# A decoder layer on one core: weight tiles of the seven-product stage that last for the stage and are loaded by halves

## The chip, the core and the metric

The kernel runs on one core of a Trainium2 chip. The metric is the device time of one execution in microseconds; the time before is the median of three runs. Times inside the execution are read from one profiled execution and counted from its start.

## What is computed

The reference is one decoder layer on 512 tokens of width 2048, all float32. Only its end matters for the change:

```python
x = layer_norm(DEEPNORM_ALPHA * x + mix, ln_mix_g[layer], ln_mix_b[layer])
f = jnp.square(jax.nn.relu(x @ w_ff1[layer])) @ w_ff2[layer]
x = layer_norm(DEEPNORM_ALPHA * x + f, ln_ff_g[layer], ln_ff_b[layer])
```

`w_ff1` is 2048 x 8192, `w_ff2` 8192 x 2048. The change touches only `x @ w_ff1`.

## The kernel before

**Precision.** Every float32 product is made of three matmuls on a faster 32-bit format: each operand is split into a high part (written by ScalarE, L87) and the rest (written by VectorE, L88), and high x high, high x low and low x high are added up in PSUM. So each weight half that TensorE uses goes through ScalarE and then VectorE first. The split parts of weights are called wh and wl; each has three buffers.

**The seven-product stage.** `x @ w_ff1` is cut into 16 groups of 512 columns. The first group is computed plainly. The other 15 are units (class `FUnit`): each takes its 2048 x 512 weights as a 2 x 2 matrix of four tiles of 1 MB, 1024 x 256 each, called "11", "12", "21" and "22", and the activations as 2 x 2 as well, and computes the product with seven block products (ORDER, M1 to M7) where eight would be plain. The price is sums of weight tiles on VectorE (`FUnit.sum`, L612), which are made in place, half a tile at a time: 11 += 12, 11 += 22, 12 += 22, 11 += 21.

**Pieces.** Each product has two pieces, one for each half of its weight tile; a unit has 14, j = 0 to 13, and a piece is 24 matmuls of 256 columns (L652). Products by piece: j 0 and 1 use "11"; 2 and 3 "11" after 11 += 12; 4 and 5 "11" after 11 += 22; 6 and 7 "22"; 8 and 9 "12" after 12 += 22; 10 and 11 "21"; 12 and 13 "11" after 11 += 21.

**The order of the work** is written out by hand. In front of the matmuls of piece j stand the split of piece j + 2 (with the sums 11 += 12 and 11 += 22 for the first four pieces) and what `beside` lists for j. That holds the sums 12 += 22 (j 4 and 6) and 11 += 21 (j 8 and 9), the evacuation of PSUM to the tile R (`block`, L661 on VectorE; L617 to L619 and L664 on ScalarE), and for the unit before: additions in R (L548) and its output to DRAM, `h_parts_out`, at j 5 and j 7. That output splits R into hpH (a high part in one buffer, ScalarE, L87) and the rest in R itself (VectorE, L88), and GpSimd's queue writes both to h_parts (L555), 896 KB each. GpSimd's queue also carries three loads of 256 KB of the other work of the stage (y_load) at j 7. Each engine and each queue runs its own instructions in the order written.

**Four tiles and their hand-over.** SBUF holds only four weight tiles at a time. When a unit has used one up, it hands its place to the next unit, whose tile is then loaded by SyncE's queue (L608, one transfer of 1 MB):

```python
        elif j == 6:
            act(u2, u.ps["M1"], AF.Copy, scale=-1.0)
            u.sum("12", "22", 1)
            u.give("22", u.order[0])
        elif j == 7:
            u.give("12", u.order[1])
```

`order` is "11", "12", "22", "21": the place of "22" takes the next "11" (at j 6), that of "12" the next "12" (j 7), that of "21" the next "22" (j 9) and that of "11" the next "21" (j 11). In the trace all these tiles are named w. The load waits until all readers of the old tile are done.

Of the kernel before, what the change touches and what calls it, by code (L numbers as in the profile page):

```python
# [9 lines left out]
F32 = mybir.dt.float32  # L10
# [6 lines left out]
P = 128  # L17
# [51 lines left out]
def decoder_layer(ctx: ExitStack, tc: tile.TileContext, x, xt, positions, w_in, w_pool, pool_scale,  # L69
                  w_branch_attn, w_branch_pool, w_out, ln_mix_g, ln_mix_b, w_ff1, w_ff2,  # L70
                  ln_ff_g, ln_ff_b, consts, vectors, out, h_parts, h_rest, y_norm, y_parts):
    nc = tc.nc
# [364 lines left out]
    L2 = {}  # L437
# [78 lines left out]
    def y_load(t, n):  # L516
        c = slice(n * 512, (n + 1) * 512)
        nc.gpsimd.dma_start(low["u"][:, 1], y_norm[t, :, c])
        nc.gpsimd.dma_start(low["g"][:, 0], bcast(ln_mix_g, c))
        nc.gpsimd.dma_start(low["g"][:, 1], bcast(ln_mix_b, c))  # L520
# [51 lines left out]
    def ff1_evac(g):  # L572

        def f(b, p):
            if not R:
# [8 lines left out]
    ORDER = ("M1", "M5", "M6", "M3", "M7", "M2", "M4")  # L584
    FACTORS = {"M1": ("11", "11"), "M5": ("P1", "11"), "M6": ("P2", "11"), "M3": ("P4", "22"), "M7": ("P3", "12"),
               "M2": ("12", "21"), "M4": ("22", "11")}
    low = {}

    def yblock(who, k):

# [7 lines left out]
    class FUnit:  # L598
# [3 lines left out]
            self.rest = None  # L602
            self.g, self.b, self.tag, self.next, self.ps, self.out = g, {}, {}, None, {}, h_out(g)

        def get(self, role):
            self.b[role] = L2["p"].tile([P, 8, 256], F32, name="w1", tag=self.tag[role])
            k, c0 = int(role[0]) - 1, self.g * 512 + (2 - int(role[1])) * 256
            nc.sync.dma_start(self.b[role], w_ff1[k * 1024:(k + 1) * 1024, c0:c0 + 256].rearrange("(a p) n -> p a n", p=P))  # L608

        def sum(self, role, other, half):  # L610
            c = slice(4 * half, 4 * half + 4)
# [6 lines left out]
                nc.scalar.activation(R[self.g][:, :, 2], self.ps["M1"].rearrange("p (n t) -> p n t", n=2), AF.Relu)  # L618
                nc.scalar.activation(R[self.g][:, :, :4], R[self.g][:, :, :4], AF.Square)  # L619

        def give(self, role, new):
            self.next.tag[new] = self.tag[role]
            self.next.get(new)

    class FPiece:
        def __init__(self, unit, j):
# [27 lines left out]
    def beside(u, j, last):  # L654

        v = {m: p.rearrange("p (n t) -> p n t", n=2) for m, p in u.ps.items()}
        m1, m5, u2 = low["m"][:, 0], low["m"][:, 1], low["u"][:, 0]
        act = nc.scalar.activation

        def block(slot, in0, in1, op):  # L660
            nc.vector.tensor_tensor(R[u.g][:, :, slot], in0.rearrange("p (n t) -> p n t", n=2), in1, op=op)  # L661

        def relu(a, b):
            act(R[u.g][:, :, a:b], R[u.g][:, :, a:b], AF.Relu)  # L664

        if j == 0:
            last.done()
        elif j == 2:
            act(m1, u.ps["M1"], AF.Copy)
        elif j == 4:  # L670
            act(m5, u.ps["M5"], AF.Copy, scale=-1.0)
            u.sum("12", "22", 0)
        elif j == 6:
            act(u2, u.ps["M1"], AF.Copy, scale=-1.0)
            u.sum("12", "22", 1)
            u.give("22", u.order[0])
        elif j == 7:
            u.give("12", u.order[1])
            if chunks:
                y_load(*chunks[0])  # L680
        elif j == 8:
            u.sum("11", "21", 0)
        elif j == 9:
            u.sum("11", "21", 1)
            u.give("21", u.order[2])
        elif j == 10:
            block(0, m5, v["M1"], OP.subtract)
        elif j == 11:
            u.give("11", u.order[3])
            if chunks:  # L690
                u.rest = y_rows(*chunks.pop(0))
        elif j == 12:
            block(1, u2, v["M5"], OP.subtract)
        elif j == 13:
            block(3, m1, v["M2"], OP.add)
            relu(0, 2)
        if j == 3 and last.rest:
            last.rest()
        if j in last.out:
            last.out[j]()  # L700
# [190 lines left out]
    units = [Unit(c, u) for c in range(7) for u in range(2)]  # L891
# [30 lines left out]
    p = PS.tile([P, 512], F32, name="mm", bufs=6)  # L922
# [170 lines left out]
```

## Time and profile before

| what | us |
|---|---|
| median of three runs | 2491.09 |
| lowest and highest of them | 2490.66, 2492.37 |
| the profiled execution | 2494.17 |
| its span in the profile | 2492.4 |
| TensorE busy in the span | 2418.1 (97%) |
| VectorE busy | 1585.7 (64%) |
| ScalarE busy | 960.9 (39%) |
| mean granted clock of TensorE | 0.985 |

The span is what lies between the first and the last instruction of the profile; 1.8 us lie around it. A busy engine is not an engine at its best: TensorE counts as busy while it runs at half its clock. So beside the busy time the granted clock and the number of matmuls in a stretch have to be read. PE is TensorE, DVE VectorE, ACT ScalarE, POOL GpSimd, SP SyncE, whose queue issues the loads of weights.

### The profile page before, as it was taken

To read this page: it belongs to the slowest core of one execution; us is meant where nothing else is said; L and a number is where in the kernel's file an instruction comes from. 1 tells how busy PE (TensorE), PEld (TensorE's weight loads), DVE (VectorE), ACT (ScalarE), POOL (GpSimd) and SP (SyncE) were. 2 spreads that over 40 slices of the span, in tenths; PEclk is the share of its full clock that TensorE was granted. 3 is DMA by queue.
4 is the path that set the end of the run, shared out by engine and by line. 5 is a ranking of instruction groups with operands and counts; after the bars stand their busy time and mean duration, and the time that the engine had idled before them with its cause. 6 is when DMAs were issued, how large, how long until landed. Compare 5 with 4: busy or idle time off the path is not lost.

```text
span 2492.4 us, 31596 instructions
## 1 busy us (share of the span) xinstructions
PE 2418.1 (97%) x13096; PEld 2101.9 (84%) x13096; DVE 1585.7 (64%) x1641; ACT 960.9 (39%) x1030; POOL 168.7 (7%) x256
## 2 busy tenths in 40 slices
PE   9999999999999999998998998999999999999998
PEld 7888888877788888888998998999988888888886
DVE  4532254555532333367877877878868889888886
ACT  4323311244422232156445545545454433333330
POOL 0000000000000000000111110111121001110000
PEclk9999999999999999999999999999999999999999
DMA  6232333322223333365676575674688566665652
GB/s 204 86 93 97 110 93 102 93 77 76 77 93 96 99 99 127 114 205 173 189 234 203 172 236 175 188 234 158 223 288 285 177 213 234 205 227 172 218 167 95
DMA packets 201919, 399.32 MB, mean 160 GB/s; under 512 B 11312, under 2 KB 73904, under 8 KB 201008
## 3 DMA queue, kind: packets, MB, share of 16 engines
q1 hardware_dynamic: 163312, 257.83, 32.2%
q0 software_dynamic: 36160, 135.28, 16.1%
q10 hardware_dynamic: 2304, 4.20, 0.5%
q8 instruction: 102, 1.67, 0.3%
q14 instruction: 41, 0.34, 0.0%
HBM read 329.11 MB, written 68.16 MB: 159 GB/s over the span
## 4 chain that ended last, share of the span: by engine, by line
PE 75%; DMA 11%; DVE 8%; issue 3%; ACT 2%; POOLq 0%; SPq 0%; DVEq 0%; ACTq 0%
PE mm L147 42%; PE pp L785 21%; DMA w<-in_w_ff 10%; PE mm L652 5%; DVE wl L88 4%; PE pp L830 3%; DVE w L612 1%; ACT wh L87 1%; DVE hpR L88 1%; DVE hpR L548 1%; PE sc L351 1%; PE tp L383 1%; DMA part<-y_parts 1%; DVE hpR L661 1%; DMA wr<-in_w_out 0%
## 5 line engine op out<-in xcount | busy, mean ns | idle before, releaser
L88 DVE TENSOR_TENSOR wl<-wr,wh 128x1024 fp32r<-128x1024 f32 (+1 forms) x228 | 277.4, 1219 | 570.6 <-ACT wh L87 569.9
L87 ACT ACTIVATE wh<-w 128x1024 fp32r<-128x1024 f32 x406 | 426.1, 1058 | 542.7 <-PE pp L785 296.3
L88 DVE TENSOR_TENSOR wl<-w,wh 128x1024 fp32r<-128x1024 f32 x406 | 494.2, 1220 | 151.7 <-ACT wh L87 149.8
L785 PE MATMUL pp<-wh,hop 128*128 128x512 f32 x1568 | 483.0, 389 | 1.2 <-ACT hpR L618 1.2
L87 ACT ACTIVATE wh<-wr 128x1024 fp32r<-128x1024 f32 (+1 forms) x228 | 240.4, 1055 | 616.1 <-PE mm L147 571.7
L147 PE MATMUL mm<-aH,wh 128*128 128x512 f32 (+1 forms) x1024 | 395.5, 386 | 1.8 <-ACT wh L87 1.8
L147 PE MATMUL mm<-aH,wl 128*128 128x512 f32 (+1 forms) x1024 | 386.8, 378 | 5.1 <-DVE wl L88 5.1
L147 PE MATMUL mm<-aL,wh 128*128 128x512 f32 (+1 forms) x1024 | 385.6, 377 | 0.0
L785 PEld LDWEIGHTS pp<-wh,hop 128*128 128x128 f32 x1568 | 294.3, 188 | 62.3 <-ACT hpR L618 1.4
L652 PE MATMUL mm<-aH,wl 128*128 128x256 f32 x960 | 285.9, 298 | 49.7 <-DVE wl L88 49.5
L785 PE MATMUL pp<-wl,hop 128*128 128x512 f32 x784 | 305.1, 389 | 0.6 <-DVE wl L88 0.6
L652 PE MATMUL mm<-aH,wh 128*128 128x256 f32 x960 | 282.3, 294 | 0.0
L652 PE MATMUL mm<-aL,wh 128*128 128x256 f32 x960 | 281.8, 294 | 0.0
L652 PEld LDWEIGHTS mm<-aH,wl 128*128 128x128 f32 x960 | 195.7, 204 | 53.9 <-DVE wl L88 53.6
L147 PEld LDWEIGHTS mm<-aH,wl 128*128 128x128 f32 x1024 | 193.0, 189 | 41.9 <-DVE wl L88 6.5
L147 PEld LDWEIGHTS mm<-aH,wh 128*128 128x128 f32 x1024 | 193.3, 189 | 40.0 <-ACT wh L87 3.0
L147 PEld LDWEIGHTS mm<-aL,wh 128*128 128x128 f32 x1024 | 193.2, 189 | 37.0 <-issue 1.9
L652 PE MATMUL mm<-ysH,wl 128*128 128x256 f32 x720 | 204.5, 284 | 3.0 <-DVE wl L88 3.0
L652 PE MATMUL mm<-ysH,wh 128*128 128x256 f32 x720 | 204.5, 284 | 0.0
L652 PE MATMUL mm<-ysL,wh 128*128 128x256 f32 x720 | 204.2, 284 | 0.0
L652 PEld LDWEIGHTS mm<-aH,wh 128*128 128x128 f32 x960 | 195.4, 204 | 0.2 <-ACT wh L87 0.2
L652 PEld LDWEIGHTS mm<-aL,wh 128*128 128x128 f32 x960 | 195.3, 203 | 0.0
(175 smaller groups left out, 3360.5 us busy)
## 6 DMA issues: line engine op xcount, KB each, us to landing
wr<-in_w_in SPq DMA_DIRECT2D x127, 512.0 KB, 3.6
w<-in_w_ff SPq DMA_DIRECT2D x60, 1024.0 KB, 15.4
w<-in_w_ff SPq DMA_DIRECT2D x112, 512.0 KB, 6.5
hop<-h_parts POOLq DMA_DIRECT2D x98, 512.0 KB, 7.1
h_parts<-hpH POOLq DMA_DIRECT2D x28, 896.0 KB, 8.2
h_parts<-hpR POOLq DMA_DIRECT2D x28, 896.0 KB, 8.9
wr<-in_w_out SPq DMA_DIRECT2D x40, 512.0 KB, 3.6
wr<-in_w_ff SPq DMA_DIRECT2D x32, 512.0 KB, 3.8
```

What stands on the lines that cost most here:

```text
L87: nc.scalar.activation(dst_h, src, AF.Copy)
L88: nc.vector.tensor_tensor(dst_l, src, dst_h.bitcast(F32), op=OP.subtract)
L147: nc.tensor.matmul(o, l, r, start=first and j == 0, stop=last and j == 2)
L351: nc.tensor.matmul(p[:, :n], qT[h][:, qb * P:(qb + 1) * P], kT[h][:, :n], start=True, stop=True)
L383: nc.tensor.matmul(p[:, k * P:], vt["v"][:, k, h * HD:(h + 1) * HD], pT[h][:, k, k * P:], start=k == 0, stop=k == 3)
L548: nc.vector.tensor_tensor(r[:, :, d], r[:, :, x0], r[:, :, x1], op=op)
L612: nc.vector.tensor_tensor(self.b[role][:, c], self.b[role][:, c], self.b[other][:, c], op=OP.add)
L652: nc.tensor.matmul(o, l, r, start=first, stop=self.j % 2 == 1 and k == 3 and i == 2, skip_group_check=True)
L661: nc.vector.tensor_tensor(R[u.g][:, :, slot], in0.rearrange("p (n t) -> p n t", n=2), in1, op=op)
L785: nc.tensor.matmul(u.ps[:, t], l, r, start=q + j == 0, stop=q == 3 and j == 2)
L830: nc.tensor.matmul(o, l, r, start=first and i == 0, stop=last and i == 2)
```

## The change

The four weight tiles are allocated once for the stage (dictionary W1, by place) and no longer anew for every unit. A load becomes two transfers of 512 KB, one for each half of the tile, and a half is handed over as soon as that half of the old tile is used up. Only the last unit's tiles, which pass to the next stage, are still handed over whole. The instructions of TensorE, VectorE and ScalarE, and their order, are the same.

```diff
-    low = {}
+    low, W1 = {}, {}
...
-        def get(self, role):
-            self.b[role] = L2["p"].tile([P, 8, 256], F32, name="w1", tag=self.tag[role])
+        def get(self, role, halves=(0, 1)):
+            tag = self.tag[role]
+            if tag not in W1:
+                W1[tag] = L2["p"].tile([P, 8, 256], F32, name="w1", tag=tag)
+            self.b[role] = W1[tag]
             k, c0 = int(role[0]) - 1, self.g * 512 + (2 - int(role[1])) * 256
-            nc.sync.dma_start(self.b[role], w_ff1[k * 1024:(k + 1) * 1024, c0:c0 + 256].rearrange("(a p) n -> p a n", p=P))
+            for h in halves:
+                r = (2 * k + h) * 512
+                nc.sync.dma_start(W1[tag][:, 4 * h:4 * h + 4],
+                                  w_ff1[r:r + 512, c0:c0 + 256].rearrange("(a p) n -> p a n", p=P))
...
-        def give(self, role, new):
+        def give(self, n, half):
+
+            role, new = ("22", "12", "21", "11")[n], self.order[n]
             self.next.tag[new] = self.tag[role]
-            self.next.get(new)
+            if self.next is not units[0]:
+                self.next.get(new, (half,))
+            elif half:
+                self.next.get(new)
...
         elif j == 4:
             act(m5, u.ps["M5"], AF.Copy, scale=-1.0)
             u.sum("12", "22", 0)
+            u.give(0, 0)
         elif j == 6:
             act(u2, u.ps["M1"], AF.Copy, scale=-1.0)
             u.sum("12", "22", 1)
-            u.give("22", u.order[0])
+            u.give(0, 1)
+            u.give(1, 0)
         elif j == 7:
-            u.give("12", u.order[1])
+            u.give(1, 1)
             if chunks:
                 y_load(*chunks[0])
         elif j == 8:
             u.sum("11", "21", 0)
+            u.give(2, 0)
         elif j == 9:
             u.sum("11", "21", 1)
-            u.give("21", u.order[2])
+            u.give(2, 1)
         elif j == 10:
             block(0, m5, v["M1"], OP.subtract)
+            u.give(3, 0)
         elif j == 11:
-            u.give("11", u.order[3])
+            u.give(3, 1)
```

How the orders stand. SyncE's queue, the loads that the first unit hands over to the second, in the order "11", "12", "22", "21" of the new unit, and the first of the third; before (the number behind w is the allocation, the names in brackets are the semaphores that a row waits for: DMAHW loads, DVE VectorE, Activation ScalarE):

```order
L608 DMA w_8053<-in_w_ff 128x8x256 [waits DMAHW4_49,DVE_49,Activation_49]
L608 DMA w_8083<-in_w_ff 128x8x256 [waits DMAHW7_49,DMAHW3_49,DVE_49]
L608 DMA w_8151<-in_w_ff 128x8x256 [waits DMAHW0_49,DMAHW5_49,DVE_49,Activation_49]
L608 DMA w_8211<-in_w_ff 128x8x256 [waits DMAHW2_49,DMAHW1_49,DVE_49]
L608 DMA w_8500<-in_w_ff 128x8x256 [waits DMAHW0_49,DVE_49,Activation_49]
```

The same place of SyncE's queue in the changed kernel, two rows for each tile, and one row of the next hand-over:

```order
L613 DMA w_7708<-in_w_ff 128x4x256 [waits DMAHW2_49,DMAHW6_49,DVE_49,Activation_49]
L613 DMA w_7708<-in_w_ff 128x4x256 [waits DMAHW3_49,DMAHW7_49,DVE_49,Activation_49]
L613 DMA w_7705<-in_w_ff 128x4x256 [waits DMAHW4_49,Activation_49]
L613 DMA w_7705<-in_w_ff 128x4x256 [waits DMAHW5_49,DVE_49]
L613 DMA w_7869<-in_w_ff 128x4x256 [waits DMAHW0_49,DVE_49,Activation_49]
L613 DMA w_7869<-in_w_ff 128x4x256 [waits DMAHW1_49,DVE_49,Activation_49]
L613 DMA w_7669<-in_w_ff 128x4x256 [waits DVE_49] x2
L613 DMA w_7869<-in_w_ff 128x4x256 [waits DMAHW2_49,DMAHW6_49,DVE_49,Activation_49]
```

Four loads have become eight, in the same order of tiles; the tiles keep their allocation (w_7708 and so on), and each half has waits and a semaphore of its own.

VectorE's queue at the end of the first unit and the start of the second: the splits of pieces 0 and 1 of the new unit, the sums 11 += 12 and the subtractions into R (hpR) of the old unit; before (DMASW are transfers of GpSimd's queue):

```order
L527 SCALAR_TENSOR_TENSOR low<-low 128x512 [waits DMASW0_49,DVE_49]
L88 TENSOR_TENSOR wl<-w_8053,wh 128x1024 [waits DMAHW6_49,PE_49,Activation_49]
L612 TENSOR_TENSOR w_8053<-w_8053,w_8083 128x1024 [waits DMAHW7_49,DMASW3_49,DVE_49]
L661 TENSOR_TENSOR hpR<-low,mm 128x2x256 [waits DMASW5_49,DMASW2_49]
L88 TENSOR_TENSOR wl<-w_8053,wh 128x1024 [waits PE_49,Activation_49]
L612 TENSOR_TENSOR w_8053<-w_8053,w_8083 128x1024 [waits DVE_49]
```

The same place of VectorE's queue in the changed kernel:

```order
L527 SCALAR_TENSOR_TENSOR low<-low 128x512 [waits DMASW0_49,DVE_49]
L88 TENSOR_TENSOR wl<-w_7708,wh 128x1024 [waits DMAHW2_49,PE_49,Activation_49]
L618 TENSOR_TENSOR w_7708<-w_7708,w_7705 128x1024 [waits DMAHW4_49,DMASW3_49,DVE_49]
L672 TENSOR_TENSOR hpR<-low,mm 128x2x256 [waits DMASW5_49,DMASW2_49]
L88 TENSOR_TENSOR wl<-w_7708,wh 128x1024 [waits DMAHW3_49,PE_49,Activation_49]
L618 TENSOR_TENSOR w_7708<-w_7708,w_7705 128x1024 [waits DMAHW5_49,DVE_49]
```

Nothing moved here; each split and each sum now waits for the load of its own half, and the subtraction into R waits for two transfers of GpSimd's queue as before.

## Rows read from the trace of the kernel before

**Rows 1.** The page, chain of work that ended last, shares of the span by engine.

```profile
PE 75%; DMA 11%; DVE 8%; issue 3%; ACT 2%; POOLq 0%; SPq 0%; DVEq 0%; ACTq 0%
```

**Rows 2.** Stretches: length, busy us and instructions by engine, clock, DMA share, GB/s.

```profile
1211.00:1825.00 614.00, 566.03 (x4479) 561.66 (x4478) 472.04 (x447) 305.63 (x307) 86.35 (x116) 0.95 0.63 202
```

**Rows 3.** Who waited for whom, 1211 to 1825 us: total, times, longest.

```profile
DVE w L612 <- DMA w<-in_w_ff: 53.3, 14, 5.6
...
PE mm L652 <- DVE wl L88: 47.9, 17, 4.7
```

**Rows 4.** Chain that ended last, 1285 to 1330 us: start, us, what.

```profile
1297.31 18.70 DMA w<-in_w_ff
...
1317.24 0.68 DVE hpR L661
...
1323.91 1.05 ACT wh L87
```

**Rows 5.** TensorE in order of time: start, us, instruction; idle before it and releaser.

```profile
1295.11 0.28 PE L652 MATMUL mm<-aH,wh 128*128 128x256 f32 x1
...
1315.40 0.28 PE L652 MATMUL mm<-aH,wh 128*128 128x256 f32 x1
1315.52 0.28 PE L652 MATMUL mm<-aL,wh 128*128 128x256 f32 x1
1319.11 0.58 PE L652 MATMUL mm<-aH,wl 128*128 128x256 f32 x1 [3.31 <-DVE wl L88]
...
1524.30 0.28 PE L652 MATMUL mm<-aH,wh 128*128 128x256 f32 x1
```

**Rows 6.** Short stretches, columns as in rows 2.

```profile
1319.10:1322.50 3.40, 3.39 (x16) 3.39 (x17) 3.37 (x4) 2.38 (x4) 0.00 (x0) 0.50 0.12 39
...
1540.00:1556.00 16.00, 12.77 (x97) 11.72 (x96) 10.66 (x10) 9.42 (x10) 0.00 (x0) 1.00 0.56 167
...
1279.00:1290.00 11.00, 11.00 (x94) 11.00 (x93) 10.90 (x13) 6.79 (x8) 0.20 (x1) 1.00 0.01 2
1291.00:1320.00 29.00, 25.69 (x210) 25.41 (x209) 20.90 (x19) 10.71 (x11) 5.49 (x8) 0.98 0.97 315
```

**Rows 7.** VectorE in order of time, around the boundary at 1315 us.

```profile
1286.97 1.21 DVE L612 TENSOR_TENSOR w<-w,w 128x1024 f32<-128x1024 f32 x1
...
1296.06 1.22 DVE L88 TENSOR_TENSOR wl<-w,wh 128x1024 fp32r<-128x1024 f32 x1 [1.21 <-ACT wh L87]
...
1324.98 1.23 DVE L88 TENSOR_TENSOR wl<-w,wh 128x1024 fp32r<-128x1024 f32 x1 [1.68 <-ACT wh L87]
```

**Rows 8.** Issues on SyncE's and GpSimd's queue, and ScalarE's second hpH split.

```profile
1290.34 0.98 POOL L555 DMA_DIRECT2D h_parts<-hpH  x1
...
1294.91 0.37 SPq L608 DMA_DIRECT2D w<-in_w_ff  x1
...
1295.93 1.69 ACT L87 ACTIVATE hpH<-hpR 128x1792 fp32r<-128x1792 f32 x1
...
1299.97 0.99 POOL L555 DMA_DIRECT2D h_parts<-hpR  x1 [1.08 <-DVE hpR L88]
...
1523.14 0.37 SPq L608 DMA_DIRECT2D w<-in_w_ff  x1
```

**Rows 9.** Issues at 1290.34, 1294.9, 1297.9, 1299.97, 1184.8, all: KB, us to landing.

```profile
h_parts<-hpH POOLq DMA_DIRECT2D x1, 896.0 KB, 4.8
...
w<-in_w_ff SPq DMA_DIRECT2D x1, 1024.0 KB, 15.3
...
h_parts<-hpH POOLq DMA_DIRECT2D x1, 896.0 KB, 12.5
...
h_parts<-hpR POOLq DMA_DIRECT2D x1, 896.0 KB, 13.3
...
w<-in_w_ff SPq DMA_DIRECT2D x1, 1024.0 KB, 5.8
...
wr<-in_w_ff SPq DMA_DIRECT2D x32, 512.0 KB, 3.8
```

## The prediction

> **What bounds the kernel now.** The chain of work that ended last comes first: TensorE 75% and DMA 11% [rows 1]. TensorE is the limit nearly everywhere, so a gain can come only from where it stands still or runs slowly. The table by stage says where that is. From 1211 to 1825 us, 13 of the 15 units of the seven-product stage, TensorE is busy 566.03 of 614 us at a granted clock of 0.95 [rows 2]. At the full clock the matmuls of the seven-product stage start 0.12 us apart (1315.40, 1315.52) [rows 5]. The 4479 of the stretch would need 4479 x 0.12 = 537.5 us and take 614: **76.5 us are lost there**, of which 614 - 566 = 48 us is standing still and 28.5 us slow matmuls.
>
> Who ends the stops: TensorE waits 47.9 us, 17 times, for VectorE's wl (the low part of a weight half), and VectorE's sum of two weight tiles (L612) waits 53.3 us, 14 times, for a transfer of w [rows 3]. That is one stop at each of the 14 boundaries between units, the first at 1220 us and the last at 1816. The one at 1315 us shows the parts. The load of the new "12" tile was issued at 1297.31 and took 18.70 us [rows 4]; TensorE stopped after 1315.52, stood for 3.31 us [rows 5], and then ran 3.4 us at clock 0.50, which is 1.2 GHz [rows 6]. A boundary with shorter stops, 1540:1556, where TensorE is busy 12.77 of 16 us, keeps 1.00 [rows 6].
>
> Why the load is late: it is issued only when a whole 1 MB tile is free, and all loads and writes of a unit are then in flight together. From 1279 to 1290 us the DMA engines do nothing (2 GB/s), from 1291 to 1320 they are full (0.97, 315 GB/s) [rows 6].
>
> **The change part by part.** I count pieces 0 to 13 in a unit; a piece is 24 matmuls, 24 x 0.12 = 2.88 us, a unit 40.32 us. T is the moment at which the second half of the sum 12+=22 ends and the first load of a unit is issued now: 1294.91 in the unit at hand [rows 8].
>
> (1) The first half of the new "11" goes out when the first half of the sum 12+=22 has ended, 1286.97 + 1.21 = 1288.18 [rows 7], that is 6.7 us before T. It then falls into the idle stretch. Its cost on the path is nothing as long as it does not delay what follows it (below).
>
> (2) At T its second half goes out and, at once, the first half of "12", whose split stands ahead of that sum. These two are 1 MB, as the "11" alone was, and that one landed in 15.3 us [rows 9]. The second half of "12" follows where the whole "12" went out before, and is half as much. Before, the second MB landed at 1297.31 + 18.70 = T + 21.1 [rows 4]; I put the middle between the two, T + 18.2. When are they wanted? In the least disturbed unit T is 1523.14 [rows 8] and piece 8 starts at 1524.30 [rows 5], T + 1.16. Piece 11 ends four pieces on, at T + 12.7; then ScalarE and VectorE split piece 0 of the next unit, which takes 2.3 us (from 1323.91 to 1324.98 + 1.23) [rows 4, 7], and the sum with "12" could start at T + 15.0. The first half is there at T + 15.3. The second is wanted some 3.1 us later (the sum 1.21, a subtraction 0.68, the next split 1.23 [rows 4, 7]), at T + 18.1, and there at T + 18.2. Each may be late by nearly a piece, 2.88 us, before TensorE sees it, since splits run two pieces ahead. So the wait for the loads **goes, almost exactly**.
>
> (3) "22" and "21" also go out by halves, the first 2 to 3 us earlier than now. Both are wanted later than "12" and the present stops are not put down to them: nothing.
>
> (4) The instructions of TensorE, VectorE and ScalarE and their order are the same, so no engine gets work. VectorE must fit into the shorter unit: 472.04 us of work in the stretch [rows 2] is 35.4 us a unit (336 of 4479 matmuls), with 1.21 + 1.68 = 2.9 us of waiting for ScalarE that a unit cannot avoid [rows 7], 38.3 of 40.32 us. It fits, with 2.0 us to spare.
>
> (5) **What is late next.** Behind the sum with "12" stands a subtraction into R, L661, and R's slots are still being written out to h_parts from the unit before. Today this write is over first: issued at 1299.97, it takes 13.3 us [rows 8, 9], so it lands at T + 18.4, and the sum waits until T + 21.1 anyway. With that wait gone, L661 waits for the write, and queued behind it on VectorE are the next split, the second sum, another subtraction, and through it ScalarE's three activations ahead of its next split. From the start of L661 to the end of the split of piece 3 this takes 1324.98 + 1.23 - 1317.24 = 8.97 us [rows 4, 7]. So that split ends at T + 27.4. TensorE wants it nine pieces after piece 8, 25.92 us: from the least disturbed unit's T + 1.16, and 0.24 us for the two matmuls that need only wh, that is T + 27.3, a stop of 0.1 us; from the unit at hand, where piece 8 starts at 1295.11, T + 0.20 [rows 5], it is T + 26.4, a stop of 1.0 us. The early half load may push the writes back by up to its own 0.5 MB at 315 GB/s, 1.7 us. Bounds per unit: 0 and 2.7 us. I take 0.7, in the middle of the two units, since the early half lies mostly in idle time. 14 x 0.7 = 10 us, with no cost in clock, because stops of this size left it at 1.00 [rows 6].
>
> The sum: -76.5 + 10 = -66.5 us. The profiled execution took 2494.17 us with a span of 2492.4; it comes to 2427.7. The median of the runs is 3.1 us below the profiled one, so 2491.1 - 66.5 = **2424.6 us**.
>
> At (2) a rule stands against the change. Two halves have the fixed part of a transfer twice: alone, 1 MB lands in 5.8 us and 512 KB in 3.8 [rows 9], so 2 x 3.8 - 5.8 = 1.8 us more per pair if it is paid in series. I take nothing, since the stretch is full at 315 GB/s with several in flight, where such parts lie side by side.
> The Trainium skill, "DMA: Bandwidth & Descriptors", section "Measured (HBM→SBUF, 128 partitions, SWDGE, issued from GpSimd)", says to batch transfers to 1 MiB or more for 75% of peak, and its section "Anatomy of one DMA — SWDGE (gpsimd) path" gives each transfer a fixed part of about 2 us; by that the loss would be an estimated 2 us per pair, 28 us for one pair on the path of 14 units. No run here shows it yet for halves of this tile in a full queue.
>
> **The rivals.**
> *Nothing is late next*: the writes land earlier too, because half a MB has left the crowd. 2491.1 - 76.5 = 2414.6. For it: T + 27.4 against T + 27.3. Against it: the early half is served beside the first write.
> *A stop stays in each unit*: the writes cost the 2.7 us of the bound, or the fixed parts are paid in series, 1.8 us for each of the one and a half pairs up to the second half of "12", 2.7 us again. Such a stop again drops the clock for 3.4 us at half, which costs 1.7. 14 x 4.4 = 62 us are given back: 2477. If the clock falls in no unit, 14 x 2.7 = 38: 2452. For it: only 2.0 us of VectorE's time a unit are free to catch up. Against it: the full queue, as in (2).
> *Slower*: ScalarE's second hpH split reuses the buffer of the first and so waits for its write. This write lands in 4.8 us while the queue is empty, and the second split starts at 1295.93, 0.8 us after 1290.34 + 4.8 [rows 8, 9]; the second write, in the crowd, takes 12.5 us [rows 9]. If the early half makes a crowd of the first as well, ScalarE stands 12.5 - 4.8 - 0.8 = 6.9 us, with the weight splits behind it. TensorE loses up to 6.9 and 1.7 in clock: 14 x 8.6 = 120, in place of 76.5, so 2491.1 + 44 = 2535. It decides where these losses reach 76.5 / 14 = 5.5 us a unit, that is from a landing of 4.8 + 0.8 + 3.8 = 9.4 us on. Against it: half a MB is 1.7 us of transfer and starts 2 us before that write.
> *The halves do not come apart*: each half load still waits for the whole old tile. Then the times stay, 2491. Against it: in the order each sum and split waits for the load of its own half, and the two loads of a tile are two rows with waits of their own.
>
> **How the numbers follow.** The forecast, with 0.1 to 1.7 us late per unit (2416 to 2438), 0.60. Nothing late next 0.14. A stop stays (2438 to 2480) 0.17. No change 0.05. Slower 0.04. The range runs from just under the second case, 2412, to 2452, the third without the fall of the clock; half of that case and the last two are left out, 0.17. A measurement of this kernel can tell 0.2%, 5 us, from no change: faster 0.91, same 0.05, slower 0.04.
>
> **What would show it.** A busy share of TensorE above 97% at a clock of 1.00 between 1211 and 1760 us; a unit in 40.3 to 42 us where it took 46 (614 us for 4479 / 336 units); the wait of the sum for w near nothing, and, if (5) holds, a wait of L661 (in the changed file L672) for the h_parts writes in its place; the first load of a unit some 6 us before the second. A wait of ScalarE's hpH for its write of more than 2 us a unit would be the slower rival; waits of the sum for w of 2 us and more would mean that (2) misjudged the landings. The forecast is wrong if the crowd of transfers moves with the earlier start instead of thinning.

## The result and the profile after

The median went from 2491.7 us to **2432.9** (four runs, 2429.76 to 2439.19), a ratio of 0.9767 with a 95% interval of 0.9747 to 0.9788: faster, as forecast, inside the range and 8 us above the predicted 2424.6. A second set of runs of the same kernel, beside the first experiments, gave 2430.8 (0.9757, 0.974 to 0.9775). The profiled execution took 2429.76 us, its span is 2428.0.

The page of the changed kernel: TensorE's busy time, and the shares of the chain that ended last, to be held against [rows 1].

```profile
PE 2392.9 (99%) x13096; PEld 2078.2 (86%) x13096; DVE 1585.5 (65%) x1641; ACT 963.1 (40%) x1030; POOL 168.7 (7%) x256
...
PE 75%; issue 11%; DMA 6%; DVE 5%; ACT 2%; POOL 1%; POOLq 0%; SPq 0%; DVEq 0%; ACTq 0%
```

The same stage by stretch, columns as in [rows 2], and below it who waited for whom from 1205 to 1770 us, to be held against [rows 3] (total, times, longest).

```profile
1211.00:1770.00 559.00, 550.61 (x4554) 547.19 (x4553) 480.24 (x454) 314.68 (x314) 90.64 (x124) 1.00 0.69 222
```

```profile
DVE w L618 <- DMA w<-in_w_ff: 18.0, 10, 2.9
...
PE mm L663 <- DVE wl L88: 8.3, 12, 1.6
...
DVE hpR L672 <- DMA h_parts<-hpR: 6.4, 6, 1.5
ACT hpH L87 <- DMA h_parts<-hpH: 5.5, 8, 1.7
```

TensorE is busy 550.61 of 559 us, 98.5%, at clock 1.00. Its 4554 matmuls would need 546.5 us at 0.12 us each, so 12.5 us are lost where 76.5 were; the difference, 64.0 us, is nearly all of the profiled gain (2494.17 - 2429.76 = 64.4). A unit takes 559 x 336 / 4554 = 41.2 us. What is left is not one wait but three: the sum's for w, the subtraction L672's for the write of R, and ScalarE's for the write of hpH.

To say at which piece TensorE stands, I take the distance from the first matmul of a piece to the first of the next, less 2.88 us, in the trace of each kernel, added over units 1 to 13 of 15 (the expectations below count the two at the edges too, which adds some tenths). Before: 70.3 us, of which 65.9 at piece 1. After: 12.2, of which **5.6 at piece 3 and 6.1 at piece 10**, and nothing at piece 1.

**Piece 3.** The unit with T = 1283.15. SyncE's queue [rows 8], each row from a window of its own, and the times from issue to landing of these four loads and of the second write of R (issued at 1288.37) [rows 9].

```profile
1276.48 0.37 SPq L613 DMA_DIRECT2D w<-in_w_ff  x1
...
1283.15 0.37 SPq L613 DMA_DIRECT2D w<-in_w_ff  x1
...
1283.62 1.47 SPq L613 DMA_DIRECT2D w<-in_w_ff  x1
...
1285.54 0.92 SPq L613 DMA_DIRECT2D w<-in_w_ff  x1
```

```profile
w<-in_w_ff SPq DMA_DIRECT2D x1, 512.0 KB, 3.6
...
w<-in_w_ff SPq DMA_DIRECT2D x1, 512.0 KB, 11.3
...
w<-in_w_ff SPq DMA_DIRECT2D x1, 512.0 KB, 15.3
...
w<-in_w_ff SPq DMA_DIRECT2D x1, 512.0 KB, 17.2
...
h_parts<-hpR POOLq DMA_DIRECT2D x1, 896.0 KB, 13.0
```

The first half of "11" goes out 6.7 us before T. "12" lands by halves at T + 15.8 and T + 19.6, the write of R at 1288.37 + 13.0 = T + 18.2. VectorE in order of time meets all three within five microseconds [rows 7], and TensorE shows what comes of it [rows 5].

```profile
1299.05 1.23 DVE L618 TENSOR_TENSOR w<-w,w 128x1024 f32<-128x1024 f32 x1 [1.10 <-DMA w<-in_w_ff]
1301.40 0.69 DVE L672 TENSOR_TENSOR hpR<-low,mm 128x512 f32<-128x512 f32 x1 [1.13 <-DMA h_parts<-hpR]
1302.01 1.22 DVE L88 TENSOR_TENSOR wl<-w,wh 128x1024 fp32r<-128x1024 f32 x1
1303.26 1.23 DVE L618 TENSOR_TENSOR w<-w,w 128x1024 f32<-128x1024 f32 x1
...
1309.16 1.23 DVE L88 TENSOR_TENSOR wl<-w,wh 128x1024 fp32r<-128x1024 f32 x1 [1.68 <-ACT wh L87]
```

```profile
1309.41 0.28 PE L663 MATMUL mm<-ysL,wh 128*128 128x256 f32 x1
1310.44 0.39 PE L663 MATMUL mm<-ysH,wl 128*128 128x256 f32 x1 [0.76 <-DVE wl L88]
```

The sum waits 1.10 us for the first half of "12", the subtraction 1.13 for the write, the second half lands 0.5 us before its sum; 2.2 us late on VectorE become 0.76 us of standing still on TensorE, and piece 3 loses 1.0 in all. Only two of the other 13 boundaries lose as much at piece 3.

**Piece 10.** Another unit. In order of time: the first write of hpH goes out on GpSimd's queue, ScalarE's second hpH split waits for it, TensorE stops. Below that, what the write took from issue to landing, and the stretch with its clock.

```profile
1359.93 0.98 POOL L555 DMA_DIRECT2D h_parts<-hpH  x1 [2.39 <-ACT hpH L87]
...
1368.38 1.70 ACT L87 ACTIVATE hpH<-hpR 128x1792 fp32r<-128x1792 f32 x1 [1.69 <-DMA h_parts<-hpH]
...
1373.32 0.39 PE L663 MATMUL mm<-aH,wl 128*128 128x256 f32 x1 [1.61 <-DVE wl L88]
```

```profile
h_parts<-hpH POOLq DMA_DIRECT2D x1, 896.0 KB, 8.4
```

```profile
1370.00:1375.00 5.00, 3.38 (x29) 3.18 (x28) 4.89 (x4) 2.45 (x4) 1.98 (x2) 1.00 0.93 266
```

The write takes 8.4 us where it took 4.8 [rows 9], the split starts 1.69 us late, and TensorE stands 1.61; the clock stays at 1.00. This is the longest first write of 13 units: read unit by unit, its median is 5.9 us here and 4.8 before. Three units with 0.7 to 1.7 us of this wait lose 3.8 of the 6.1 us at piece 10; two others lose 2.2, one of them (the unit shown at piece 3) without any wait for the write, so a part of this stop has another cause, which was not looked for.

### The profile page after: what moved, and what is told of

It reads as the page before. It is cut to its first block, busy times and chain, and to the rows that moved or that the text cites. A ratio compares the mean times of both kernels' runs of the same rounds, so it can differ in the third digit from the quotient of the medians.

```text
span 2428.0 us, 31729 instructions
## 1 busy us (share of the span) xinstructions
PE 2392.9 (99%) x13096; PEld 2078.2 (86%) x13096; DVE 1585.5 (65%) x1641; ACT 963.1 (40%) x1030; POOL 168.7 (7%) x256
## 4 chain that ended last, share of the span: by engine, by line
PE 75%; issue 11%; DMA 6%; DVE 5%; ACT 2%; POOL 1%; POOLq 0%; SPq 0%; DVEq 0%; ACTq 0%
PE mm L147 43%; PE pp L800 20%; PE mm L663 5%; PE pp L845 4%; DMA w<-in_w_ff 2%; DVE wl L88 2%; DMA h_parts<-hpH 2%; DMA h_parts<-hpR 1%; DVE hpR L88 1%; PE sc L351 1%; PE tp L383 1%; ACT wh L87 1%; DMA low<-in_ln_mix_g 1%; ACT hpH L87 1%; DMA wr<-in_w_out 0%
## 5 line engine op out<-in xcount | busy, mean ns | idle before, releaser
L663 PE MATMUL mm<-aH,wl 128*128 128x256 f32 x960 | 273.0, 284 | 7.0 <-DVE wl L88 7.0
L663 PE MATMUL mm<-aH,wh 128*128 128x256 f32 x960 | 271.9, 283 | 0.0
L663 PE MATMUL mm<-aL,wh 128*128 128x256 f32 x960 | 271.9, 283 | 0.0
L147 PEld LDWEIGHTS mm<-aH,wl 128*128 128x128 f32 x1024 | 193.5, 189 | 41.7 <-DVE wl L88 6.3
L147 PEld LDWEIGHTS mm<-aH,wh 128*128 128x128 f32 x1024 | 193.7, 189 | 39.1 <-ACT wh L87 2.5
L147 PEld LDWEIGHTS mm<-aL,wh 128*128 128x128 f32 x1024 | 193.8, 189 | 36.9 <-issue 1.9
L663 PEld LDWEIGHTS mm<-aH,wl 128*128 128x128 f32 x960 | 184.3, 192 | 8.7 <-DVE wl L88 8.4
L663 PEld LDWEIGHTS mm<-aH,wh 128*128 128x128 f32 x960 | 184.5, 192 | 0.0
L663 PEld LDWEIGHTS mm<-aL,wh 128*128 128x128 f32 x960 | 184.4, 192 | 0.0
## 6 DMA issues: line engine op xcount, KB each, us to landing
w<-in_w_ff SPq DMA_DIRECT2D x232, 512.0 KB, 10.8
```

The source lines that it names most:

```text
L147: nc.tensor.matmul(o, l, r, start=first and j == 0, stop=last and j == 2)
L663: nc.tensor.matmul(o, l, r, start=first, stop=self.j % 2 == 1 and k == 3 and i == 2, skip_group_check=True)
```

## The experiments

All of them side by side. "Unit" is 559 x 336 over the count of matmuls from 1211 to 1770 us (40.32 is the floor), the waits are from the same stretch (us, times), "at 1, 3, 10" is what TensorE loses at these pieces in 13 units (at piece 2 run 4 loses another 3.4, run 7 4.3 and run 9 7.1; at piece 7 run 11 loses 3.9). "Wait for w" is that of VectorE's sum alone: where the new "11" comes whole or late, ScalarE's split waits for it too (57.8 us before, 52.4 in run 2, 24.2 in run 7, 43.8 in run 8), but piece 0 loses at most 2.1 us in any run. The kernel before had medians of 2491.4, 2492.0 and 2494.5 in the three groups (1 to 4, 5 to 8, 9 to 12), so across groups the ratios count.

| run | median us | ratio (95%) | unit | wait for w | L672 for R | hpH | at 1, 3, 10 |
|---|---|---|---|---|---|---|---|
| changed, again | 2430.8 | 0.9757 (0.974-0.9775) | 41.4 | 16.6, 11 | 12.3, 11 | 4.1, 5 | 1.5, 6.7, 5.1 |
| 2 tiles alone | 2492.5 | 1.0003 (0.9994-1.0013) | 45.9 | 48.1, 13 | - | 1.1, 2 | 62.1, 2.2, 0 |
| 3 halves at the old lines | 2432.7 | 0.9765 (0.9747-0.9782) | 41.6 | 17.0, 14 | 13.4, 11 | 5.1, 7 | 1.5, 8.5, 5.7 |
| 4 "11" alone by halves | 2459.7 | 0.9874 (0.9856-0.9891) | 43.1 | 50.5, 13 | - | 3.7, 3 | 15.2, 11.4, 5.6 |
| 5 R's write frees R | 2428.1 | 0.9742 (0.9728-0.9757) | 41.1 | 23.6, 15 | - | 3.2, 6 | 0.6, 7.1, 2.1 |
| 6 both writes free | 2417.0 | 0.9701 (0.9685-0.9717) | 40.3 | 2.5, 2 | - | - | 0, 0, 0 |
| 7 first half held | 2459.0 | 0.9868 (0.9853-0.9883) | 42.8 | 51.6, 14 | - | 0.2, 1 | 15.0, 11.1, 1.7 |
| 8 "12" alone by halves | 2470.7 | 0.9919 (0.9904-0.9934) | 44.6 | 37.2, 13 | - | 0.4, 1 | 41.9, 7.8, 1.4 |
| 9 waits on 64 bytes | 2450.3 | 0.982 (0.9805-0.9836) | 42.4 | 44.5, 20 | 1.2, 1 | - | 4.3, 14.1, 1.6 |
| 10 quarters | 2424.9 | 0.9717 (0.9697-0.9737) | 40.8 | 18.3, 14 | 6.1, 5 | 0.9, 2 | 0, 3.9, 2.1 |
| 11 first hpH at 4 | 2441.5 | 0.9783 (0.9762-0.9803) | 42.0 | 11.1, 9 | 25.4, 13 | 3.6, 4 | 5.8, 9.8, 2.1 |
| 12 that, y loads at 8 | **2419.3** | 0.9695 (0.968-0.971) | 40.3 | - | - | 2.2, 3 | 0, 0, 0 |

### What of the change makes the gain

**The changed kernel again.** 

> The changed kernel once more, as the measure for the other runs on the same chip. All theories: 2430 to 2439 us, as measured. In its stage from 1211 to 1770 us the lost time was 559 - 4554 x 0.12 = 12.5 us in the profiled execution, and waits for h_parts writes (L672 6.4 us, the hpH split 5.5 us) and for w (18.0 us, not all of it seen by TensorE) should stand there again.

It repeats; its waits for R are twice those of the first profile (12.3 against 6.4 us), with the same loss at piece 3. So the split between the waits of VectorE varies from execution to execution more than what TensorE loses.

**2: the tiles alone.** Lasting tiles, but one transfer of 1 MB and a whole hand-over.

```diff
-            for h in halves:
-                r = (2 * k + h) * 512
-                nc.sync.dma_start(W1[tag][:, 4 * h:4 * h + 4],
-                                  w_ff1[r:r + 512, c0:c0 + 256].rearrange("(a p) n -> p a n", p=P))
+            nc.sync.dma_start(W1[tag], w_ff1[k * 1024:(k + 1) * 1024, c0:c0 + 256].rearrange("(a p) n -> p a n", p=P))
...
-            if self.next is not units[0]:
-                self.next.get(new, (half,))
-            elif half:
+            if half:
```

> The tiles last for the stage, but each is loaded by one transfer of 1 MB and handed over whole, at the places of the kernel before. Theory 'halves' (the gain comes from the loads and hand-overs by halves, the allocation does nothing): 2491, as before, with one stop of TensorE of 3 to 5 us a unit and a fall of its clock. Rival 'allocation' (a lasting tile frees the loads of waits that a new allocation brings): well under 2491, near 2432.

The kernel before in all respects; its waits from 1211 to 1770 us read like [rows 3]:

```profile
DVE w L615 <- DMA w<-in_w_ff: 48.1, 13, 5.3
...
PE mm L658 <- DVE wl L88: 42.2, 17, 4.4
```

The allocation is worth nothing; the halves are worth all.

**3: halves, issued at the old lines.** Both halves of a tile stand where the whole load stood.

```diff
-            if self.next is not units[0]:
-                self.next.get(new, (half,))
-            elif half:
+            if half:
                 self.next.get(new)
```

> Loads of 512 KB, with the consumers waiting for their own half, but both halves issued when the whole old tile is free, at the places of before (T, T + 2.4, T + 9.4, T + 12.2). Theory 'landing by halves' (it is enough that a consumer waits for its half): the first half of 12 should land near T + 18, the second near T + 21; sums wanted at T + 15 and T + 18 are late by 3 us, which the 2.9 us of lead cover almost, so some 0.5 to 2 us a unit: 2435 to 2450. Theory 'early issue' (the loads must start in the idle stretch): most of the old stop is back, 2470 or more.

This was no test. SyncE's queue carries nothing else here, and its rows and their waits come out the same: a load goes out when its waits are met, wherever its line stands. The first half was issued at the same time as in the changed kernel (1276.48 there):

```profile
1276.49 9.63 SPq L613 DMA_DIRECT2D w<-in_w_ff  x4
```

It shows only that of the change the new places of `give` bring nothing beyond the transfers of halves. Run 7 is the test that this one failed to be.

**4: only the new "11" by halves**, the other three whole.

```diff
+            if halves == (0, 1):
+                nc.sync.dma_start(W1[tag], w_ff1[k * 1024:(k + 1) * 1024, c0:c0 + 256].rearrange("(a p) n -> p a n", p=P))
+                return
...
-            if self.next is not units[0]:
+            if self.next is not units[0] and n == 0:
```

> Only the place that becomes the new 11 is handed over and loaded by halves, its first half early; the other three tiles are 1 MB at the old places. Theory 'early issue': 0.5 MB less in the crowd, the 12 lands whole near T + 19.6 instead of T + 21.1, a stop of some 2 us a unit: 2450 to 2465. Theory 'landing by halves' (the 12 must come by halves): nearly the old stop, 2475 or more.

Half of the gain, 31.7 us of 60.6. The sum still waits for w, 50.5 us, now for a "12" of 1 MB.

**7: the early half held back until T.** A 64-byte transfer out of the second half of "12" stands ahead of both halves of "11" on SyncE's queue.

```diff
-            if self.next is not units[0]:
+            if self.next is units[0]:
+                if half:
+                    self.next.get(new)
+            elif n:
                 self.next.get(new, (half,))
             elif half:
+                nc.sync.dma_start(out[:1, :16], self.b["12"][:1, 4, :16])
                 self.next.get(new)
```

> The first half of the new "11" is held back on SyncE's queue by a 64-byte transfer out of the tile "12" as its second half is summed, so that it goes out at T with the second half (the 16 numbers that it writes into the first row of the output are written over later). All else is as in the changed kernel. If the 0.5 MB moved 6.7 us ahead into the idle stretch is what makes the loads land in time, they land 0.5 MB at about 315 GB/s, 1.7 us, to 6.7 us later: 14 units lose 1 to 5 us each, 2445 to 2490, and the sum's wait for w is 30 us or more. If landing and waiting by halves is what counts, and the moment of issue not, the time stays at 2429 to 2434.

28 us slower than the changed kernel, by the ratios as by the medians: the early half matters. SyncE's queue there, in one piece (x5 are the loads from the first on):

```profile
1287.82 0.26 SPq L637 DMA_DIRECT2D out<-w  x1
1288.19 12.19 SPq L613 DMA_DIRECT2D w<-in_w_ff  x5
```

The price is an upper bound, since three loads, not two, now queue up at T, and the later halves leave SyncE later too; what the 64-byte transfer itself costs is in it as well (run 9 below has four of them a unit, on the other queue, and is slowed).

**8: only the new "12" by halves.** The counterpart of run 4, with the same lines in `get`.

```diff
...
-            if self.next is not units[0]:
+            if self.next is not units[0] and n == 1:
```

> Only the new "12" is loaded by halves, at the places of the changed kernel; "11", "22" and "21" are 1 MB transfers issued when the whole old tile is free. Of the two parts of step (2) this keeps the wait by halves for "12" and leaves out the early half of "11" ("11" alone by halves gave 2459.7). If the wait by halves on "12" carries the larger share, 2435 to 2450; if the early half and the halves of "12" add up, 31.8 us from "11" alone and about 28 us from "12" alone make 2463; if both are needed together, 2475 to 2491.

21.3 us. With run 4's 31.7 that is 53.0 of the 60.6: the early half of "11" (step 1) and the halves of "12" (step 2) add up to most of the gain, and the rest comes with "22" and "21" by halves, or with the parts together; that was not separated.

### What holds the last 12 us

**5: the write of R takes its bytes elsewhere.** So R can be rewritten at once, with the same traffic.

```diff
-        for e, v in enumerate((h.bitcast(F32), r[:, 1:])):
+        for e, v in enumerate((h.bitcast(F32), sums["P1"][1].bitcast(F32)[:, :7])):
```

> The write of R into h_parts takes the same number of bytes at the same place in the queue, but from a tile of the first matrix's sums that nobody rewrites in this stage (so the R part of h_parts is not the reference's). The subtraction into R (L672) then has no write to wait for, and the traffic stays. If that wait is the stop at piece 3 (6.8 us of the stage's 14.5 in the second run of the changed kernel), the stop at piece 3 falls below 2 us and the time by 5 to 7 us, to 2424 to 2426 beside about 2431; the stop at piece 10 stays at 4 to 7 us. If the landing of the loads sets piece 3 and the write only comes last beside it, the sum's wait for w grows by what the other loses and the time stays within 2 us of 2431.

The first theory fails. L672 waits no more, but piece 3 loses as much as before, 7.1 us, and the sum's wait for w grew from 16.6 to 23.6 us, as the second theory has it. The time is 2.7 us lower, a little beyond the second theory's 2 us, with the loss at piece 10 down from 5.1 to 2.1 (why was not looked for), and the intervals of the two kernels overlap. So R's write hid a lateness of the loads that costs piece 3 as much.

The first profile of the changed kernel, read boundary by boundary, agrees: at the three boundaries where VectorE waits for R's write alone, 1.2 to 1.5 us, piece 3 loses 0.0 to 0.3 us; at the five where it waits 2.3 to 2.9 us for w alone, 0.5 to 1.1. In the second profile the two waits mostly stand at the same boundary and add up, and one wait for R alone, of 1.8 us, goes with a loss of 0.6.

**6: both writes take their bytes elsewhere.**

```diff
-        for e, v in enumerate((h.bitcast(F32), r[:, 1:])):
+        for e, v in enumerate((sums["P1"][0].bitcast(F32)[:, :7], sums["P1"][1].bitcast(F32)[:, :7])):
```

> Both writes into h_parts, of R and of hpH, take as many bytes from tiles that nobody rewrites in this stage (h_parts is then not the reference's). If the two stops are the wait of the subtraction into R and that of ScalarE's second hpH split, both go: piece 3 and piece 10 together lose 10 to 12 us, and the time is 2417 to 2421, close to the 2414.6 of the case in which nothing is late next. If the stop at piece 10 has another cause, it stays at 4 to 7 us and the time is that of the run that frees R alone, 2424 to 2426. If the loads are what is late, 2430.

The stretch has no loss left, and the time is that of "nothing late next" (2414.6 forecast, 2417.0 measured):

```profile
1211.00:1770.00 559.00, 559.00 (x4660) 558.96 (x4659) 492.05 (x462) 322.76 (x319) 95.27 (x132) 1.00 0.70 226
```

The issues of w in the same stretch (count, KB each, median us from issue to landing):

```profile
w<-in_w_ff SPq DMA_DIRECT2D x109, 512.0 KB, 4.8
```

But it changed more than the two waits. These writes wait for no engine, so GpSimd sends them, and the y loads that stand between them on its queue, far ahead of the computation in most units. The crowd after T is gone there: a half load lands in 4.8 us (median), in the changed kernel in 12.0. It shows that the last 12 us hang on GpSimd's transfers behind T, and not on which of them, nor whether by the waits for them or by the crowd.

**9: the waits shortened, the crowd kept.** Before each big write, 64 bytes go out of the tile that is rewritten; the big write takes its bytes elsewhere. So L672 and the second hpH split wait for 64 bytes, and the big writes still start when hpH and R are ready.

```diff
         for e, v in enumerate((h.bitcast(F32), r[:, 1:])):
+            n = 32 * j + 16 * e
+            nc.gpsimd.dma_start(out[:1, n:n + 16], v[:1, 0, :16])
+            v = sums["P1"][e].bitcast(F32)[:, :7]
```

> Each write into h_parts is now two: first 64 bytes of the rewritten tile (hpH or R) into the first row of the output, which is written over later, then the full number of bytes from a tile that nobody rewrites (h_parts is then not the reference's). So the big writes go out at the moments of the changed kernel, 0.5 us later each, with the same crowd, but ScalarE's second hpH split and the subtraction into R (L672) wait only for the 64 bytes. If these waits are the stops: both go, 2417 to 2421 as with the writes that wait for nothing (2417.0). If the loads of w end just as late at piece 3 (freeing R alone gave only 2.7 us): the stop at piece 10 falls below 1 us, that at piece 3 stays at 5 to 8 us, 2424 to 2428. If neither wait matters: 2430.

None of the theories: 16 us slower than the changed kernel by the ratios (0.982 against 0.9757), 19.5 by the medians. The waits for the writes are gone but for one of 1.2 us, and piece 10 is down to 1.6; but the loads land later, and so VectorE waits longer for w. The waits from 1211 to 1770 us, and the issues of the same stretch (KB each, median us to landing):

```profile
DVE w L621 <- DMA w<-in_w_ff: 44.5, 20, 4.1
```

```profile
w<-in_w_ff SPq DMA_DIRECT2D x107, 512.0 KB, 14.1
...
out<-hpH POOLq DMA_DIRECT2D x26, 0.1 KB, 6.0
out<-hpR POOLq DMA_DIRECT2D x26, 0.1 KB, 8.4
```

So piece 3 stops without the waits for the writes too, and loses 14.1 us: a late landing of "12" in the crowd is enough. And that landing is sensitive: with four transfers of 64 bytes more per unit the median half load lands 2 us later (14.1 against 12.0). Why so much was not settled; each takes GpSimd's queue 0.5 us, which moves the writes behind them.

**11: the first hpH split one piece earlier.**

```diff
-                5: lambda: h_parts_out(g, 0), 7: lambda: h_parts_out(g, 1)}
+                4: lambda: h_parts_out(g, 0), 7: lambda: h_parts_out(g, 1)}
```

> The first hpH split, its subtraction and its two writes come one piece earlier, at piece 4 in place of 5; the second stays at 7. The first hpH write then has 2.9 us more before ScalarE's second split waits for it: this wait (5.5 us in the changed kernel's profile, 8 times) falls to zero and the stop at piece 10 (5 to 6 us) below 1 us; also a first write that is over earlier thins the crowd: 2423 to 2428. If the split at piece 4 only moves work of VectorE (1.7 us) ahead of a weight split that TensorE wants: a new stop of 0.3 us or more per unit, 2430 to 2436.

Piece 10 went down to 2.1 us, but in 13 units TensorE now loses 23.3 us where the two profiles of the changed kernel have 12.2 and 14.4. The median is higher too, but the intervals of the ratios overlap. Two things cost. One is the second theory of the expectation: the split of hpH at piece 4 puts VectorE's work ahead of a weight split, and piece 7 loses 3.9 us, 0.3 a unit. In one of these units:

```profile
1286.21 0.39 PE L663 MATMUL mm<-ysH,wl 128*128 128x256 f32 x1 [0.96 <-DVE wl L88]
```

The other I had not named, and it comes at two of the 14 boundaries. GpSimd's queue in order of time shows it in the same unit, with the second write of R, issued at 1296.88, from issue to landing below.

```profile
1285.32 0.56 POOL L531 DMA_DIRECT2D y_parts<-low  x1 [0.34 <-DVE low L527]
1294.03 0.55 POOL L518 DMA_DIRECT2D low<-y_norm  x1 [8.15 <-DMA y_parts<-low]
...
1296.88 0.99 POOL L555 DMA_DIRECT2D h_parts<-hpR  x1
```

```profile
h_parts<-hpR POOLq DMA_DIRECT2D x1, 896.0 KB, 12.2
```

There the write of y_parts stands behind the first pair of writes; the y load waits 8.15 us for it, and the second pair stands behind that load. With T = 1288.49 the write of R lands at T + 20.6, and L672 waits 4.1 us, 5.2 at the other of the two boundaries; behind them pieces 1 to 3 lose 6.8 us together. **At these two boundaries the wait of step (5) is the one that bounds**: "12" had landed by T + 9.4, earlier than anywhere in the changed kernel, since the three y loads and the second pair of writes went out only after its loads. At the other boundaries of this run the y loads go out before T, "12" lands by halves from T + 13.6 on, as in the changed kernel, and the waits for w and for R stand side by side as there.

**12: the same, and the y loads at piece 8**, behind the second pair of writes, and their use at piece 13 in place of 11 (not at 12, as the expectation has it).

```diff
         elif j == 7:
             u.give(1, 1)
-            if chunks:
-                y_load(*chunks[0])
         elif j == 8:
             u.sum("11", "21", 0)
             u.give(2, 0)
+            if chunks:
+                y_load(*chunks[0])
...
         elif j == 11:
             u.give(3, 1)
-            if chunks:
-                u.rest = y_rows(*chunks.pop(0))
         elif j == 12:
             block(1, u2, v["M5"], OP.subtract)
         elif j == 13:
             block(3, m1, v["M2"], OP.add)
             relu(0, 2)
+            if chunks:
+                u.rest = y_rows(*chunks.pop(0))
```

> As the run with the earlier first hpH split, and the three y loads (0.75 MB) are issued at piece 8, behind the second pair of writes, and used at piece 12 in place of 11. The second writes then have three transfers of 256 KB less ahead of them, about 2.4 us at 315 GB/s, and so have the loads of w issued after T. If piece 3 waits for the end of this crowd, its stop (6 to 7 us) falls below 2 us: 2417 to 2422, the best version. If the y loads only change places with the rest and VectorE then waits for them at piece 12, 2426 to 2440.

The best version, faster than both kernels: 2419.3 us, 0.9695 of the time before. TensorE never stands still in the stretch:

```profile
1211.00:1770.00 559.00, 559.00 (x4661) 559.00 (x4660) 491.86 (x463) 322.82 (x320) 95.77 (x133) 1.00 0.72 230
```

The loads after T and the second write of R in one unit (T = 1279.01; issued at 1279.01, 1279.49, 1281.41 and 1284.07), from issue to landing:

```profile
w<-in_w_ff SPq DMA_DIRECT2D x1, 512.0 KB, 5.7
...
w<-in_w_ff SPq DMA_DIRECT2D x1, 512.0 KB, 7.5
w<-in_w_ff SPq DMA_DIRECT2D x1, 512.0 KB, 7.6
...
h_parts<-hpR POOLq DMA_DIRECT2D x1, 896.0 KB, 9.8
```

"12" is there at T + 8.0 and T + 10.0, the write is over at T + 14.9: 7.8, 9.6 and 3.3 us earlier than in the unit shown of the changed kernel, with the same bytes in a unit. The medians of 13 units say the same: T + 7.8, T + 9.5 and T + 14.9, where the changed kernel has T + 15.6, T + 19.1 and T + 18.2. What moved is which transfers stand between T and the loads. That it is the y loads shows against run 11, from which this run differs in the place of their issue and use alone: there the medians are T + 15.2 and T + 18.6 for "12". The y loads moved alone, with the first hpH split left at piece 5, were not run.

### Is the fixed part of a transfer paid?

**10: quarters.** Every half load is two transfers of 256 KB; who waits for what stays.

```diff
-            for h in halves:
-                r = (2 * k + h) * 512
+            for q in (2 * h + i for h in halves for i in range(2)):
+                r = (4 * k + q) * 256
-                nc.sync.dma_start(W1[tag][:, 4 * h:4 * h + 4],
-                                  w_ff1[r:r + 512, c0:c0 + 256].rearrange("(a p) n -> p a n", p=P))
+                nc.sync.dma_start(W1[tag][:, 2 * q:2 * q + 2],
+                                  w_ff1[r:r + 256, c0:c0 + 256].rearrange("(a p) n -> p a n", p=P))
```

> Every half load is issued as two transfers of 256 KB at the same place, with nothing waiting for a quarter alone. If the fixed part of a transfer is paid in series (1.8 us per pair, the rival at step (2)), three more transfers stand ahead of the end of the second half of "12": 5.4 us per unit, at least 14 x (5.4 - 2) = 48 us and the clock falls again: 2475 to 2510. If the parts lie side by side in the full queue: 2428 to 2436.

Not slower but about 0.4% faster than the changed kernel (0.9717 with an upper end of 0.9737; the changed kernel's intervals begin at 0.974 and 0.9747). A quarter lands in 9.7 us (median), where a half took 12.0; but a half is there only with its later quarter:

```profile
w<-in_w_ff SPq DMA_DIRECT2D x214, 256.0 KB, 9.7
```

Read unit by unit, the halves of "12" are there at T + 15.9 and T + 18.8 (medians of 13 units), as in the changed kernel (T + 15.6 and T + 19.1), so for them nothing is paid and nothing gained. The second write of R lands at T + 17.2 where it was T + 18.2, and no first hpH write takes more than 6.1 us where the longest took 8.4. Why was not tried further.

The rule of the Trainium skill that was weighed at step (2) ("DMA: Bandwidth & Descriptors", "Measured (HBM→SBUF, 128 partitions, SWDGE, issued from GpSimd)": batch to 1 MiB or more) would have it the other way round, an estimated 28 us more for halves by the fixed part of about 2 us of the same page's section "Anatomy of one DMA — SWDGE (gpsimd) path", and more than that for quarters. In this full queue of SyncE nothing of it is seen.

## Why the prediction was right, and where it was not

**What bounds the kernel**: right. Of the 76.5 us lost in the stretch 64.0 came, and run 12, in which the stretch loses nothing, gains 75 (2494.5 to 2419.3).

**(1)** Right: the first half goes out 6.7 us before T, to the tenth, and by run 7 it is worth up to 28 us.

**(2)** Right in kind, a little early in number. Forecast T + 15.3 and T + 18.2, measured T + 15.8 and T + 19.6; the chain no longer stops at piece 1. But the waits for w are 18.0 us, 10 times, not "near nothing", and five of the ten reach 2 us, the prediction's own sign that (2) misjudged the landings; the medians of 13 units are T + 15.6 and T + 19.1. None is much above the 2.88 us of lead (the longest is 2.9), so TensorE sees only a part of each, up to 1.1 us at piece 3. That the fixed part costs nothing in this queue is borne out by run 10.

**(3), (4)** Right: all ten waits for w are for "12", none for "22" or "21", and the clock stayed at 1.00. VectorE's fit is tight and does not bind: with every stop gone (runs 6 and 12) it is busy 492 of 559 us.

**(5)** The mechanism is in the trace as described: the write of R lands at T + 18.2 (forecast 18.4), from the start of L672 to the end of the split of piece 3 it takes 1310.39 - 1301.40 = 8.99 us (8.97), and piece 3 loses 1.0 us there, 0.76 of it standing still (0.1 to 1.0). Two things were missed. First, it is not alone, and in the first profile not the wait that costs most: the loads of "12" arrive as late, the boundaries with a wait for R alone lose 0.0 to 0.3 us there, and taking that wait away gains nothing at piece 3 (run 5). Only at the two boundaries of run 11, where the write is later and the loads early, does it bound. Over 13 units piece 3 lost 5.6 / 13 = 0.4 us a unit, where 0.7 were taken. Second, a term was missing: **ScalarE's wait for the first hpH write**. The prediction had it only as the slower rival, with 6.9 us per unit if the write takes 12.5. It takes 5.9 us in the median and 8.4 at most, 4.8 before; the 0.8 us to spare are used up, and ScalarE waits 5.5 us in all, 8 times. Piece 10, where most of this shows, lost 6.1 / 13 = 0.5 us a unit. The two errors nearly cancel: 12.5 us in place of 10. So the sum is close by luck in part, 0.3 us a unit too much at piece 3 and 0.5 too little at piece 10.

**The time.** The profiled execution came to 2429.76 where the sum says 2427.7. The other 6 us of the 8 are in the step to the median: the profile before lay 3.1 us above its median, that after 3.1 below. One execution does not tell on which side of the median the next kernel's will lie; that belongs into the range.

**The rivals.** "Nothing late next", 2414.6, did not come by itself; run 12 comes near it, at 2419.3, by another order of GpSimd's queue. "A stop stays" with 2.7 us per unit did not come. "Slower" named the wait that came, but at 5.5 / 13 = 0.4 us a unit, below the 2 us of its sign. "The halves do not come apart" is the kernel that run 2 builds, at 2492.5.

## What to carry to other kernels

Where a transfer stops an engine, look first at what else is in flight between its issue and its landing: the halves gained 60 us mostly by sending bytes into an idle stretch and by waiting for less, and moving three loads that are not wanted soon behind the others, with one pair of writes put earlier, gave 11 more by the medians, 15 by the ratios. When two transfers of one crowd land within a microsecond or two of each other, taking away the wait for one shows the other, so price the crowd and not the wait. And an issue that waits on a queue holds all that stand behind it: check every queue in which a step is moved, as run 11 shows.

## What was not expected of the hardware

A transfer of 64 bytes on GpSimd's queue took 6.0 and 8.4 us (medians, run 9) from issue to landing in the crowd, as long as a 512 KB load took behind T in the unit shown of run 12 (5.7 to 7.6). The loads of SyncE's queue and the transfers of GpSimd's slow each other: the second half of "11" takes 11.3 us (median of 13 units) with three y loads issued around it, 10.8 in run 11, and 6.0 in run 12, which differs from run 11 only in having these behind it; and the first hpH write takes 5.9 with a half load beside it, 4.8 before. The Trainium skill has a rule for this ("DMA: Bandwidth & Descriptors", "Queues, rings and completion order": each DMA engine goes round between the queues that it has work for, a packet at a time); these rows agree with it and do not prove it. Stops of up to 1.6 us left the granted clock at 1.00 all through the stage, where the stop of 3.31 us before was followed by 0.50 [rows 5, 6]. In between it went both ways: a stop of 2.14 us (run 7, at 1352.5) was followed by 0.50 for 3.4 us, one of 2.56 (run 4, at 1309.6) was not.
